# Queueing the joins of the FFN's transposed words behind the weight cast traced last

## The chip, the cores and the metric

The kernel runs on one core of one Trainium2 chip. The metric is the device time of one execution in microseconds (us). An execution starts with the inputs in the chip's memory and ends with the output there. "PE" is TensorE, "DVE" VectorE, "ACT" ScalarE, "POOL" GpSimd and "SP" SyncE, which in this kernel issues the DMAs.

## The reference, cut to what matters

Two layers of an encoder on one sequence of 256 tokens with width 1024 are computed in float32. Each layer has two attention branches, a merge, a gated feed-forward net (FFN) and an embedding per layer. The change touches the FFN alone, whose hidden width is 2816:

```python
u  = rms_norm(h, g_ffn_pre)                 # 256 x 1024
gu = u @ w_ffn_in                           # 256 x 5632: gate | up
h  = h + rms_norm((silu(gate) * up) @ w_ffn_out, g_ffn_post)
```

## The kernel before, in words

**Precision.** A float32 product is made of three products of a reduced type. Each operand is kept as a rounded part ("hi") and the rest ("lo"), and PE adds hi·hi, hi·lo and lo·hi. `split(hi, lo, src)` makes the two parts: ACT casts (L112), DVE subtracts (L108). Each weight of the net passes through it on its way: SP loads a unit of 1 MB into a buffer (raw, two of them; some weights go to "lent" or "big" buffers), ACT casts it to wh, DVE subtracts to wl and thereby frees the raw buffer for the next load, and PE uses both in 12 or 24 matmuls of 128x512. The class `Stream` (`ws`) does this. At most four units are held as wh and wl (`depth`): a cast waits until PE has done with the unit whose buffer it takes, and the casts and subtractions are traced from `done`, that is, right after PE's work on an older unit is traced.

**The FFN.** The hidden width is worked in blocks of 256. The first part makes blocks singly (`block`, a weight for both halves of the tokens). Six blocks are made in three pairs (`pair`, `seven`): the seven products of a fast 2x2 scheme instead of eight. For it DVE makes sums of weights in place in the lent buffers (`add` in `step`, L289). A step n of a pair uses one weight x, y, z, q or a sum of them, so a step needs its load, for some steps one of the sums, a cast and a subtraction. The products themselves are added and subtracted on ACT and DVE (L617, L621, L624, L626). The order of units is the string `FFN = "uu1u2u34u567" "uo12o34o5o67" "poo12o345o67"`: u is a unit of a single block, a digit a step of a pair, o an output unit of w_ffn_out, p the loads for the end of the layer. So the second and the third pair are mixed with output units.

**The transposes.** The hidden values come out as tokens x width, and the output product needs width x tokens. In the FFN this goes by a DMA. `turn_words` copies the 16-bit words of the float32 values apart on ACT (L401), SP issues a transposing DMA (L407), ACT joins the words again in two copies for a block (L413) or in one for half a pair (L419), and `self.put` splits the result (ACT cast, DVE subtraction). It is a generator: a task that runs along. At each `tick()` of the main program the open tasks may go one step on, so the joins are traced some steps after the DMA. There are eleven such transposes in each FFN.

**The order of the work.** The Python program's order isn't the order of the engines' queues. The recorded instructions go through a scheduler of the language, which sets each engine's order by its own estimates of when an operand is ready. Each engine then works through its queue in order and waits at an instruction whose operand isn't there. `tc.issue_after(x)` makes the instructions traced under it stand behind x. On one engine this is a matter of queue order alone, with no semaphore. The kernel uses it in other places already (for instance L442, L469, L526).

In the profile, names like wh_0ffnin stand for all tiles of that kind and part of the program: 0 is the first layer, ffnin the first part of the FFN. Where a text needs one tile, it is told by the number that the program gives it, as in the listings of the change below: wh_0ffnin_2964, or wh_2964 for short.

Of the kernel before, what the change touches and what calls it, by code (L numbers as in the profile page):

```python
# [18 lines left out]
P = 128  # L19
T = 256  # L20
# [30 lines left out]
def trunk_kernel(ctx: ExitStack, tc: tile.TileContext, a: dict, out: bass.AP):  # L51
# [7 lines left out]
    nc = tc.nc  # L59
# [17 lines left out]
    def big(dt=F32):  # L77
        return bigp.tile([P, 2048], dt, tag="big", name=nm("big"))

    def mid(dt=F32):  # L80
        return b4p.tile([P, 1024], dt, tag="mid", name=nm("mid"))
# [7 lines left out]
    def t512():  # L89
        return smp.tile([P, 512], F32, tag="t512", name=nm("t512"), bufs=7)  # L90
# [16 lines left out]
    def vsub(out, in0, in1):  # L107
        nc.vector.tensor_tensor(out=out, in0=in0, in1=in1, op=ALU.subtract)  # L108

    def split(hi, lo, src):  # L110

        nc.scalar.copy(hi, src)  # L112
        vsub(lo, src, hi.bitcast(F32))


    h = cp.tile([P, 2, D], F32, tag="h", name="h")
# [93 lines left out]
    class Stream:  # L210
# [70 lines left out]

        def made(self, x):
            for piece in self.put(x):
                split(*piece)

        def step(self, n, x, y, z, q):
            def add(to, other):
# [18 lines left out]
        def fill(self):  # L306
            while self.open and self.held < self.depth and self.jobs:
                pieces = self.jobs.pop(0)()
                for piece in pieces or ():
                    split(*piece)  # L310
                if pieces:
                    self.load()

# [9 lines left out]
    ws = Stream(4)  # L323
# [36 lines left out]
    class Split:  # L360
# [26 lines left out]
        def put(self, src, k, n, t0, tn):  # L387

            split(*self.at(k, n, t0, tn), src.rearrange("p (k t) -> p k t", t=tn))

        def turn_words(self, src, k, n, hf=None, far=False):

            x = lambda: t512()[:, : n * P * (2 if hf is None else 1)]
            w = x()
            w16 = w.bitcast(U16)  # L400
            nc.scalar.copy(  # L401
                w16.rearrange("p (s c) -> p s c", s=2), src.bitcast(U16).rearrange("p (c s) -> p s c", s=2)
            )
            yield SENT
            r, z = [t[:, : n * P * (2 if hf is None else 1)] for t in halves(mid())] if far else (x(), None)
            r16 = r.bitcast(U16)
            nc.sync.dma_start_transpose(out=r16.rearrange("p (r t) -> p r t", t=P), in_=w16)  # L407
            yield LANDED
            z = x() if z is None else z
            z16 = z.bitcast(U16)  # L410
            if hf is None:
                for i in range(2):
                    nc.scalar.copy(  # L413
                        z16.rearrange("p (k h t s) -> p h s k t", k=2, h=2, s=2)[:, i],
                        r16.rearrange("p (s h k t) -> p h s k t", h=2, k=2, s=2)[:, i],
                    )
                self.put(z, k, n, 0, T)
            else:
                nc.scalar.copy(z16.rearrange("p (c s) -> p s c", s=2), r16.rearrange("p (s c) -> p s c", s=2))  # L419
                self.put(z, k, n, hf * P, P)  # L420

        def tok(self, k, hf):
            return [t[:, 0, :] for t in self.at(k, 1, hf * P, P)]
# [68 lines left out]
    def halves(t):  # L492
        return [t[:, j * 512 : (j + 1) * 512] for j in range(2)]
# [88 lines left out]
    def sums(x):  # L582

        made = []

        def make():  # L590
            yield 1
            (a11, a12), (a21, a22) = x
            s2 = t512()
            vsub(a22, a21, a22)
            vsub(s2, a22, a11)
            nc.vector.tensor_tensor(out=a12, in0=a12, in1=s2, op=ALU.add)
            yield 1
            vsub(a21, a11, a21)
            for s in (a22, s2, a12, a21):
                parts = halves(mid(F32R))  # L600
                split(*parts, s)
                made.append([p.rearrange("p (k t) -> p k t", t=P) for p in parts])
                yield 1

        return made, Task(make(), part[0])

    def seven(sp, forms, gated, last):

        made, task = forms
        quad = lambda hf, j: lambda k: sp.tok(4 * j + k, hf)  # L610
        form = lambda i: lambda k: [p[:, k, :] for p in made[i]]
# [191 lines left out]
    for l in range(DEPTH):  # L803
# [219 lines left out]
        for x in range(2):  # L1023
            o = project_t(uT)
            for i in range(2):
                dst = qk[:, x, 2 * i : 2 * i + 2, :]
                src = o[i].rearrange("p (h t) -> p h t", t=T)
# [165 lines left out]
        for br in range(2):  # L1193
            t = big().rearrange("p (s c) -> p s c", s=2)
# [130 lines left out]
        for x in FFN:  # L1325
# [7 lines left out]
            if x == "o":  # L1333
                n, w = outs.pop(0), ws.take()
# [32 lines left out]
        for hf in range(2):  # L1367
            s = slice(hf * P, (hf + 1) * P)
# [85 lines left out]
```

## Time and profile before

| | us |
|---|---|
| median of three runs | 933.96 |
| the three runs | 930.89, 933.96, 934.84 |
| the profiled execution | 932.07 |
| its span (first to last instruction) | 930.4 |
| PE busy | 911.5 (98%) |
| DVE busy | 721.4 (78%) |
| ACT busy | 622.8 (67%) |

The span is the time from the first to the last instruction that the profiler saw, and the profiled execution took 1.67 us more than that. The FFN of layer 0 lies at about 263 to 440 us, that of layer 1 at 719 to 895 us; the first pair comes at about 300 to 330 us (layer 1: 755 to 785), the second at 330 to 375 and the third at 375 to 415. In rows of a timeline the columns are start, duration, engine, line, operation, out<-in, shape, and in brackets the idle time of the engine before the instruction and what ended it. Rows of waits give the sum, the number of times and the longest. "xN" is a group of N instructions of a kind that follow one another.

### The profile page before, as it was taken

What the parts mean: (1) busy time and instruction counts of PE and PEld (TensorE: products, weight loads), DVE (VectorE), ACT (ScalarE), POOL (GpSimd) and SP (SyncE); (2) the same over time, 40 slices, a digit from 0 to 9 for tenths busy, and PEclk for the clock granted to TensorE, in tenths of its full rate; (3) what the DMA queues carried; (4) which work ended last, traced back from release to release, by engine and by line L of the source; (5) the groups of instructions that cost most, each with busy time, mean ns of one, the idle gap of its engine ahead of it and who ended that gap; (6) DMA issues with size and microseconds to landing.
All of it is one profiled execution on the core that took longest, in us unless ns stands there. A gap on an engine that the chain in (4) does not pass through costs nothing.

```text
span 930.4 us, 12115 instructions
## 1 busy us (share of the span) xinstructions
PE 911.5 (98%) x4577; PEld 770.7 (83%) x4577; DVE 721.4 (78%) x871; ACT 622.8 (67%) x952; POOL 84.6 (9%) x150
## 2 busy tenths in 40 slices
PE   9999999999999989999999999999999998999996
PEld 7998888888878777888899988888888787788786
DVE  5798977656569798898689789665566797989874
ACT  5569678735477776667765686785545876857663
POOL 3500211100000000000123002100001000000000
PEclk9999999999999999999999999999999999999998
DMA  7464456857376665846555525396664856765551
GB/s 250 150 227 135 138 180 179 290 188 211 97 250 212 204 217 185 276 145 239 174 182 181 182 91 161 123 273 214 205 213 143 271 174 203 238 232 174 181 181 46
DMA packets 119896, 177.11 MB, mean 190 GB/s; under 512 B 35159, under 2 KB 58199, under 8 KB 119838
## 3 DMA queue, kind: packets, MB, share of 16 engines
q1 hardware_dynamic: 119838, 176.34, 59.1%
q8 instruction: 36, 0.59, 0.3%
q14 instruction: 22, 0.18, 0.1%
HBM read 167.41 MB, written 1.05 MB: 181 GB/s over the span
## 4 chain that ended last, share of the span: by engine, by line
PE 82%; ACT 5%; DMA 4%; DVE 4%; issue 3%; POOL 2%; SPq 0%; POOLq 0%; DVEq 0%; ACTq 0%
PE acc_1ffnin L96 10%; PE acc_0ffnin L96 9%; PE acc_1ffnin L573 5%; PE acc_1gate L96 5%; PE acc_0gate L96 5%; PE acc_1merge L96 5%; PE acc_0merge L96 5%; PE acc_0ffnin L573 4%; PE acc_1gqk L96 2%; PE acc_0gqk L96 2%; PE acc_0rq L96 2%; PE acc_1ple L96 2%; PE acc_0gg L96 2%; PE acc_1gg L96 2%; PE acc_1v L96 2%
## 5 line engine op out<-in xcount | busy, mean ns | idle before, releaser
L96 PE MATMUL acc_1ffnin<-wh_1ffnin,big_1ffnin 128*128 128x512 f32 x176 | 56.6, 392 | 0.0
L96 PE MATMUL acc_0ffnin<-wh_0ffnin,big_0ffnin 128*128 128x512 f32 x176 | 56.1, 391 | 0.0
L108 DVE TENSOR_TENSOR wl_1ffnin<-raw_1ffnin,wh_1ffnin 128x1024 fp32r<-128x1024 f32 (+1 forms) x26 | 43.9, 1713 | 6.5 <-ACT wh_1ffnin L112 6.4
L108 DVE TENSOR_TENSOR wl_0ffnin<-raw_0ffnin,wh_0ffnin 128x1024 fp32r<-128x1024 f32 (+1 forms) x26 | 43.8, 1713 | 6.0 <-ACT wh_0ffnin L112 5.6
L112 ACT CAST wh_0ffnin<-raw_0ffnin 128x1024 fp32r<-128x1024 f32 (+1 forms) x26 | 36.8, 1450 | 16.7 <-DMA raw_0ffnin<-in_w_ffn_out_dram 14.1
L112 ACT CAST wh_1ffnin<-raw_1ffnin 128x1024 fp32r<-128x1024 f32 (+1 forms) x26 | 37.0, 1447 | 16.1 <-DMA raw_1ffnin<-in_w_ffn_out_dram 6.9
L108 DVE TENSOR_TENSOR wl_0ffnin<-lent_0ffnin,wh_0ffnin 128x2048 fp32r<-128x2048 f32 (+1 forms) x19 | 34.6, 1839 | 7.9 <-ACT wh_0ffnin L112 7.9
L108 DVE TENSOR_TENSOR wl_1ffnin<-lent_1ffnin,wh_1ffnin 128x2048 fp32r<-128x2048 f32 (+1 forms) x19 | 34.6, 1838 | 7.8 <-ACT wh_1ffnin L112 7.8
L96 PEld LDWEIGHTS acc_1ffnin<-wh_1ffnin,big_1ffnin 128*128 128x128 f32 x176 | 33.0, 188 | 7.1 <-ACT big_1ffnin L112 0.2
L96 PEld LDWEIGHTS acc_0ffnin<-wh_0ffnin,big_0ffnin 128*128 128x128 f32 x176 | 33.0, 188 | 7.1 <-ACT big_0ffnin L112 0.3
L112 ACT CAST wh_0ffnin<-lent_0ffnin 128x2048 fp32r<-128x2048 f32 (+1 forms) x19 | 29.2, 1551 | 8.1 <-DVE lent_0ffnin L289 3.3
L96 PE MATMUL acc_1ffnin<-wl_1ffnin,big_1ffnin 128*128 128x512 f32 x88 | 34.3, 390 | 0.0
L96 PE MATMUL acc_0ffnin<-wl_0ffnin,big_0ffnin 128*128 128x512 f32 x88 | 34.2, 390 | 0.0
L112 ACT CAST wh_1ffnin<-lent_1ffnin 128x2048 fp32r<-128x2048 f32 (+1 forms) x19 | 29.1, 1549 | 7.5 <-DVE lent_1ffnin L289 3.1
L573 PE MATMUL acc_0ffnin<-wh_0ffnin,mid_0ffnin 128*128 128x512 f32 x96 | 31.3, 392 | 0.6 <-ACT wh_0ffnin L112 0.6
L573 PE MATMUL acc_1ffnin<-wh_1ffnin,mid_1ffnin 128*128 128x512 f32 x96 | 31.3, 392 | 0.5 <-ACT wh_1ffnin L112 0.5
L96 PE MATMUL acc_0ffnin<-wh_0ffnin,big_0wout 128*128 128x512 f32 x96 | 30.4, 390 | 0.0
L96 PE MATMUL acc_1ffnin<-wh_1ffnin,big_1wout 128*128 128x512 f32 x96 | 30.4, 389 | 0.0
L108 DVE TENSOR_TENSOR wl_1gate<-raw_1gate,wh_1gate 128x1024 fp32r<-128x1024 f32 x14 | 16.5, 1222 | 15.2 <-ACT wh_1gate L112 15.2
L108 DVE TENSOR_TENSOR wl_0gate<-raw_0gate,wh_0gate 128x1024 fp32r<-128x1024 f32 x14 | 17.2, 1273 | 11.8 <-ACT wh_0gate L112 11.7
L573 PE MATMUL acc_1ffnin<-wh_1ffnin,big_1wout 128*128 128x512 f32 x72 | 23.5, 392 | 2.5 <-DVE mid_1ffnin L108 2.5
L573 PE MATMUL acc_0ffnin<-wh_0ffnin,big_0wout 128*128 128x512 f32 x72 | 23.5, 392 | 2.4 <-DVE mid_0ffnin L108 2.3
(659 smaller groups left out, 2970.2 us busy)
## 6 DMA issues: line engine op xcount, KB each, us to landing
raw_0ffnin<-in_w_ffn_out_dram SPq DMA_DIRECT2D x11, 1024.0 KB, 5.6
raw_1ffnin<-in_w_ffn_out_dram SPq DMA_DIRECT2D x11, 1024.0 KB, 4.9
lent_0ffnin<-in_w_ffn_in_dram SPq DMA_DIRECT2D x6, 1024.0 KB, 7.4
lent_1ffnin<-in_w_ffn_in_dram SPq DMA_DIRECT2D x6, 1024.0 KB, 5.8
raw_0rq<-in_w_in_dram SPq DMA_DIRECT2D x4, 1024.0 KB
raw_0v<-in_w_in_dram SPq DMA_DIRECT2D x4, 1024.0 KB
raw_0gg<-in_w_in_dram SPq DMA_DIRECT2D x4, 1024.0 KB, 5.0
raw_0gate<-in_w_o_gla_dram SPq DMA_DIRECT2D x4, 1024.0 KB, 5.3
```

What stands on the lines that cost most here:

```text
L96: return nc.tensor.matmul(o, lhsT, rhs, start=start, stop=stop)
L108: nc.vector.tensor_tensor(out=out, in0=in0, in1=in1, op=ALU.subtract)
L112: nc.scalar.copy(hi, src)
L573: nc.tensor.matmul(o, x, y, start=first and k + n == 0, stop=k == 3 and n == 2, skip_group_check=not first)
```

## The change

`split` returns its ACT cast, and `Stream` keeps the cast of the last weight unit traced (`ws.cast`). In `turn_words` the joins and the split behind them are traced under `tc.issue_after(ws.cast.ins)`, where `far` is set, which is the case for the FFN's transposes. No instruction is added or taken away.

```diff
     def split(hi, lo, src):
-        nc.scalar.copy(hi, src)
+        cast = nc.scalar.copy(hi, src)
         vsub(lo, src, hi.bitcast(F32))
+        return cast
...
         def made(self, x):
             for piece in self.put(x):
-                split(*piece)
+                self.cast = split(*piece)
...
                 for piece in pieces or ():
-                    split(*piece)
+                    self.cast = split(*piece)
...
             z16 = z.bitcast(U16)
-            if hf is None:
-                for i in range(2):
-                    nc.scalar.copy(...)
-                self.put(z, k, n, 0, T)
-            else:
-                nc.scalar.copy(...)
-                self.put(z, k, n, hf * P, P)
+            with tc.issue_after(ws.cast.ins) if far else nullcontext():
+                if hf is None:
+                    for i in range(2):
+                        nc.scalar.copy(...)
+                    self.put(z, k, n, 0, T)
+                else:
+                    nc.scalar.copy(...)
+                    self.put(z, k, n, hf * P, P)
```

The lines of the program move by one or two (L413 is L415 in the changed kernel, L419 is L421, L289 is L290). The scheduler changes the orders of ACT, DVE and PE at several places of both FFNs, in both layers alike. The numbers of the tiles are the same in both programs.

Place A: ACT's queue in layer 0 at the first pair's steps 6 and 7. wh_2931 is the cast of step 6, wh_2964 that of step 7, wh_2968 that of a single block's unit, wh_3011 that of an output unit; mid_2922 holds the words of a single block. Before:

```order
L112 CAST wh_0ffnin_2931<-raw_0ffnin_2796 128x2048
L413 COPY mid_0ffnin_2922<-mid_0ffnin_2922 128x2x2x128 x2
L112 CAST wh_0ffnin_2964<-lent_0ffnin_2589 128x2048
L112 CAST big_0ffnin_2882<-mid_0ffnin_2922 128x2x256
L112 CAST wh_0ffnin_2968<-raw_0ffnin_2889 128x2048
L112 CAST wh_0ffnin_3011<-raw_0ffnin_2962 128x2048
```

And with the change:

```order
L112 CAST wh_0ffnin_2931<-raw_0ffnin_2796 128x2048
L112 CAST wh_0ffnin_2964<-lent_0ffnin_2589 128x2048
L112 CAST wh_0ffnin_2968<-raw_0ffnin_2889 128x2048
L415 COPY mid_0ffnin_2922<-mid_0ffnin_2922 128x2x2x128 x2
L112 CAST wh_0ffnin_3011<-raw_0ffnin_2962 128x2048
L112 CAST big_0ffnin_2882<-mid_0ffnin_2922 128x2x256
```

The two join copies have moved from ahead of two weight casts to behind them, and their own cast to big_2882 behind a third.

Place B: DVE's queue in layer 0 at the second pair's steps 3 to 6. wl_3141 is step 3, wl_3161 step 4, wl_3195 an output unit, wl_3214 step 5, wl_3232 the next output unit, wl_3262 step 6; the line L289 or L290 into lent_2972 with raw_3117 makes the sum for step 7; big_3136 and big_3191 are parts of transposed hidden values. Before:

```order
L108 TENSOR_TENSOR big_0ffnin_3136<-mid_0ffnin_3050,big_0ffnin_3136 128x4x128
L108 TENSOR_TENSOR big_0ffnin_3136<-mid_0ffnin_3064,big_0ffnin_3136 128x4x128
L108 TENSOR_TENSOR wl_0ffnin_3141<-lent_0ffnin_2972,wh_0ffnin_3140 128x2048
L108 TENSOR_TENSOR wl_0ffnin_3161<-big_0ffnin_2974,wh_0ffnin_3160 128x2048
L108 TENSOR_TENSOR big_0ffnin_3191<-mid_0ffnin_3105,big_0ffnin_3191 128x2x256
L108 TENSOR_TENSOR wl_0ffnin_3195<-raw_0ffnin_3015,wh_0ffnin_3194 128x2048
L289 TENSOR_TENSOR lent_0ffnin_2972<-lent_0ffnin_2972,raw_0ffnin_3117 128x2048
L108 TENSOR_TENSOR wl_0ffnin_3214<-lent_0ffnin_2976,wh_0ffnin_3213 128x2048
L108 TENSOR_TENSOR mid_0ffnin_3120<-acc_0ffnin_3122,mid_0ffnin_3120 128x512
L108 TENSOR_TENSOR wl_0ffnin_3232<-raw_0ffnin_3198,wh_0ffnin_3231 128x2048
L108 TENSOR_TENSOR wl_0ffnin_3262<-raw_0ffnin_3117,wh_0ffnin_3261 128x2048
L108 TENSOR_TENSOR mid_0ffnin_3119<-mid_0ffnin_3119,acc_0ffnin_3121 128x512
```

And with the change:

```order
L108 TENSOR_TENSOR big_0ffnin_3136<-mid_0ffnin_3050,big_0ffnin_3136 128x4x128
L108 TENSOR_TENSOR wl_0ffnin_3141<-lent_0ffnin_2972,wh_0ffnin_3140 128x2048
L290 TENSOR_TENSOR lent_0ffnin_2972<-lent_0ffnin_2972,raw_0ffnin_3117 128x2048
L108 TENSOR_TENSOR big_0ffnin_3136<-mid_0ffnin_3064,big_0ffnin_3136 128x4x128
L108 TENSOR_TENSOR wl_0ffnin_3161<-big_0ffnin_2974,wh_0ffnin_3160 128x2048
L108 TENSOR_TENSOR big_0ffnin_3191<-mid_0ffnin_3105,big_0ffnin_3191 128x2x256
L108 TENSOR_TENSOR wl_0ffnin_3195<-raw_0ffnin_3015,wh_0ffnin_3194 128x2048
L108 TENSOR_TENSOR wl_0ffnin_3214<-lent_0ffnin_2976,wh_0ffnin_3213 128x2048
L108 TENSOR_TENSOR mid_0ffnin_3120<-acc_0ffnin_3122,mid_0ffnin_3120 128x512
L108 TENSOR_TENSOR mid_0ffnin_3119<-mid_0ffnin_3119,acc_0ffnin_3121 128x512
L108 TENSOR_TENSOR wl_0ffnin_3232<-raw_0ffnin_3198,wh_0ffnin_3231 128x2048
L108 TENSOR_TENSOR wl_0ffnin_3262<-raw_0ffnin_3117,wh_0ffnin_3261 128x2048
```

The sum with raw_3117 has moved from behind wl_3195 to ahead of big_3136's second half and wl_3161, and the subtraction into mid_3119 from behind wl_3262 to ahead of wl_3232. The third pair has the same exchange between wl_3457 (step 3), the sum of lent_3288 with raw_3338 and wl_3477 (step 4).

On ACT, the stretch beside place B now reads like this, from step 3's cast (wh_3140) to that of the output unit (wh_3194), with step 4's cast (wh_3160) between:

```order
L112 CAST wh_0ffnin_3140<-lent_0ffnin_2972 128x2048
L421 COPY mid_0ffnin_3064<-mid_0ffnin_3064 128x2x512
L112 CAST wh_0ffnin_3160<-big_0ffnin_2974 128x2048
L112 CAST big_0ffnin_3136<-mid_0ffnin_3064 128x4x128
L415 COPY mid_0ffnin_3105<-mid_0ffnin_3105 128x2x2x128 x2
L112 CAST wh_0ffnin_3194<-raw_0ffnin_3015 128x2048
```

Before, the three copies stood ahead of wh_3140, and only one cast of hidden values (big_3191 from mid_3105) stood between wh_3160 and wh_3194. PE's order there changes too: four matmuls of the output unit (wh_3194) stand after step 3 and the first matmul of step 4, ahead of the rest of step 4; before, they stood behind all of step 4.

More of the change, by code (lines that the diff above doesn't have):

```diff
@@ L410, in turn_words @@
             z16 = z.bitcast(U16)
-            if hf is None:
-                for i in range(2):
[L413 to L416, printed above, removed]
-                self.put(z, k, n, 0, T)
-            else:
-                nc.scalar.copy(z16.rearrange("p (c s) -> p s c", s=2), r16.rearrange("p (s c) -> p s c", s=2))
-                self.put(z, k, n, hf * P, P)
+            with tc.issue_after(ws.cast.ins) if far else nullcontext():
+                if hf is None:
+                    for i in range(2):
+                        nc.scalar.copy(
+                            z16.rearrange("p (k h t s) -> p h s k t", k=2, h=2, s=2)[:, i],
+                            r16.rearrange("p (s h k t) -> p h s k t", h=2, k=2, s=2)[:, i],
+                        )
+                    self.put(z, k, n, 0, T)
+                else:
+                    nc.scalar.copy(z16.rearrange("p (c s) -> p s c", s=2), r16.rearrange("p (s c) -> p s c", s=2))
+                    self.put(z, k, n, hf * P, P)
         def tok(self, k, hf):
```

## The prediction

> **What bounds the kernel now.** I read the page's busy table first, then the waits of PE, then the timelines of the places at which PE waited.
>
> ```profile
> span 930.4 us, 12115 instructions
> PE 911.5 (98%) x4577; PEld 770.7 (83%) x4577; DVE 721.4 (78%) x871; ACT 622.8 (67%) x952; POOL 84.6 (9%) x150
> ```
>
> PE is busy for 98% of the span, so no change of order can win more than the time in which PE waits. The waits of PE (line, releaser: us in total, times, longest) say where these are:
>
> ```profile
> PE acc_1ffnin L573 <- DVE mid_1ffnin L108: 2.5, 1, 2.5
> PE acc_0ffnin L573 <- DVE mid_0ffnin L108: 2.3, 1, 2.3
> ...
> PE acc_0ffnin L573 <- ACT wh_0ffnin L112: 0.6, 1, 0.6
> ...
> PE acc_1ffnin L573 <- ACT wh_1ffnin L112: 0.5, 1, 0.5
> ```
>
> All four lie in the two FFNs, where joins, casts and subtractions share ACT and DVE. I call the first kind stall A and the second stall B.
>
> **Stall A.** The timeline at the first pair's steps 6 and 7 in layer 0, rows of all engines:
>
> ```profile
> 315.38 0.50 PE L96 MATMUL acc_0ffnin<-wl_0ffnin,big_0wout 128*128 128x512 f32 x1 [0.17 <-DVE wl_0ffnin L108]
> ...
> 320.49 0.39 PE L96 MATMUL acc_0ffnin<-wh_0ffnin,big_0wout 128*128 128x512 f32 x1
> ...
> 322.43 1.40 ACT L413 COPY mid_0ffnin<-mid_0ffnin 128x512 uint16<-128x512 uint16 x2 [3.87 <-DMA mid_0ffnin<-t_0ffnin]
> 323.70 1.90 ACT L112 CAST wh_0ffnin<-lent_0ffnin 128x2048 fp32r<-128x2048 f32 x1
> ...
> 325.63 2.29 DVE L108 TENSOR_TENSOR wl_0ffnin<-lent_0ffnin,wh_0ffnin 128x2048 fp32r<-128x2048 f32 x1 [4.74 <-ACT wh_0ffnin L112]
> 327.84 0.68 DVE L108 TENSOR_TENSOR mid_0ffnin<-mid_0ffnin,acc_0ffnin 128x512 f32<-128x512 f32 x1
> ...
> 327.95 0.92 SPq L259 DMA_DIRECT2D lent_0ffnin<-in_w_ffn_in_dram  x2
> 328.66 0.47 PE L573 MATMUL acc_0ffnin<-wh_0ffnin,big_0wout 128*128 128x512 f32 x1 [2.34 <-DVE mid_0ffnin L108]
> ```
>
> ACT stood 3.87 us before the join of mid_0ffnin_2922, until the transposing DMA had landed. Queued behind it: step 7's cast wh_2964, DVE's subtraction of it, the small subtraction that frees step 7's accumulator, and SP's loads for the next pair, whose buffer the same subtraction frees.
>
> **Place A after the change.** The casts wh_2964 and wh_2968 stand ahead of this join. wh_2964 can't start at 318.56, when ACT falls idle (322.43 − 3.87), though: it takes a buffer that PE reads until 320.88 (the row at 320.49 and its 0.39). Small waits just before, such as the one at 315.38, go too (a join stood ahead of those casts as well); I put them at 0.45, an estimate, so I start the cast at 320.45, 3.25 earlier than 323.70. Subtraction, accumulator and loads follow by as much: loads at 324.7, and step 7's wait of PE is gone. That is 2.34 of idle and 0.25 of refill, 2.6; with the 0.45, PE is 3.05 ahead. The join now lands in a gap of ACT behind the casts, and its own reader comes over 20 us later: it costs nothing.
>
> **Place B, the second pair's steps 3 and 4 and the out unit behind them:**
>
> ```profile
> 347.49 2.29 DVE L289 TENSOR_TENSOR lent_0ffnin<-lent_0ffnin,big_0ffnin 128x2048 f32<-128x2048 f32 x1
> ...
> 352.46 1.92 ACT L112 CAST wh_0ffnin<-big_0ffnin 128x2048 fp32r<-128x2048 f32 x1
> 352.61 2.29 DVE L108 TENSOR_TENSOR wl_0ffnin<-lent_0ffnin,wh_0ffnin 128x2048 fp32r<-128x2048 f32 x1 [1.64 <-ACT wh_0ffnin L112]
> 353.49 0.39 PE L573 MATMUL acc_0ffnin<-wh_0ffnin,mid_0ffnin 128*128 128x512 f32 x1
> 354.43 0.50 PE L573 MATMUL acc_0ffnin<-wh_0ffnin,mid_0ffnin 128*128 128x512 f32 x1 [0.56 <-ACT wh_0ffnin L112]
> 354.96 0.50 PE L573 MATMUL acc_0ffnin<-wl_0ffnin,mid_0ffnin 128*128 128x512 f32 x1
> 355.30 0.64 PE L573 MATMUL acc_0ffnin<-wh_0ffnin,mid_0ffnin 128*128 128x512 f32 x2
> ```
>
> From 353.49 to 355.30 stand three matmuls that at the usual pitch of 0.227 take 0.68: 1.13 lost. Afterwards, with a DVE that is 3.2 ahead: the sum that step 3 needs ends at 346.5 (it ended at 349.78), wh_3140 is cast until 348.5, wl_3141 is there at 350.85. PE comes at 353.49 − 3.05 = 350.44 and waits 0.3 to 0.4. It then has step 3's matmuls to 353.5 and one of wh_3160, and stands at 353.75 before four of wh_3194. On ACT that cast now comes last of a row: wh_3140 to 348.4, a join of 1.36, wh_3160 to 351.5, a 0.5 cast, the two block joins (1.40 in the row at 322.43), then wh_3194 from 353.25 to 355.17. PE waits 1.5, to 355.25. So B costs 1.85 where it cost 1.13. From there 47 matmuls (12 + 24 + 12 less the one done) lead to wh_3231: 355.25 + 47 × 0.227 = 365.9, against 368.28 before (the four at 368.28 are counted back from the row at 369.41 below). PE is still 2.4 ahead.
>
> **Where this is given back: the out unit wh_3231.**
>
> ```profile
> 357.63 2.28 DVE L108 TENSOR_TENSOR wl_0ffnin<-raw_0ffnin,wh_0ffnin 128x2048 fp32r<-128x2048 f32 x1
> 359.83 2.28 DVE L289 TENSOR_TENSOR lent_0ffnin<-lent_0ffnin,raw_0ffnin 128x2048 f32<-128x2048 f32 x1
> ...
> 359.94 0.37 SPq L259 DMA_DIRECT2D raw_0ffnin<-in_w_ffn_out_dram  x1
> ...
> 365.11 3.72 ACT L112 CAST wh_0ffnin<-raw_0ffnin 128x2048 fp32r<-128x2048 f32 x2 [4.87 <-DMA raw_0ffnin<-in_w_ffn_out_dram]
> 367.05 4.49 DVE L108 TENSOR_TENSOR wl_0ffnin<-raw_0ffnin,wh_0ffnin 128x2048 fp32r<-128x2048 f32 x2 [2.13 <-ACT wh_0ffnin L112]
> ...
> 369.41 0.48 PE L96 MATMUL acc_0ffnin<-wl_0ffnin,big_0ffnin 128*128 128x512 f32 x1
> ```
>
> This is a chain without slack: wl_3195 ends (359.91) and frees a raw buffer, SP issues the load (359.94), 5.17 us later ACT casts, DVE subtracts to 369.34, and PE's first matmul on wl_3232 stands at 369.41. PE's lead is worth what this chain is earlier, and no more. In the new order of DVE the sum lent_2972 += raw_3117 (2.2 by pitch) stands ahead of wl_3195 instead of behind it. So: wl_3141 to 350.85, sum to 353.05, 0.6 for big_3136, wl_3161 to 355.85, 0.6 for big_3191, wl_3195 to 358.7. The load goes out at 358.75, 1.2 earlier and not 3.2. Cast from 363.95 to 365.85; a small subtraction that now stands ahead of wl_3232 waits for PE's accumulator, closed at 365.9 by the 47 matmuls, and takes until 366.75; wl_3232 to 369.05. PE reads it at 369.1: of 2.4 only **0.3** is left. (If the small subtraction did not hold it, 1.2: the other end.)
>
> **The third pair, steps 3 to 5:**
>
> ```profile
> 397.15 1.92 ACT L112 CAST wh_0ffnin<-lent_0ffnin 128x2048 fp32r<-128x2048 f32 x1 [0.20 <-DVE lent_0ffnin L289]
> ...
> 401.30 2.29 DVE L108 TENSOR_TENSOR wl_0ffnin<-big_0ffnin,wh_0ffnin 128x2048 fp32r<-128x2048 f32 x1
> ...
> 404.47 0.39 PE L573 MATMUL acc_0ffnin<-wl_0ffnin,mid_0ffnin 128*128 128x512 f32 x1
> ...
> 418.07 0.62 PE L573 MATMUL acc_0ffnin<-wh_0ffnin,big_0wout 128*128 128x512 f32 x2
> ```
>
> Before, wl_3477 ended at 403.59, 0.88 ahead of PE's use at 404.47. In the new order the sum lent_3288 += raw_3338 and a 0.6 subtraction stand ahead of it (+2.8), while wl_3457 starts some 0.4 to 0.6 earlier (its cast no longer has a join before it, and waits for DVE's sum alone): wl_3477 ends at 405.8 ± 0.15. PE goes on at 405.85 with 58 matmuls to the one that stood at 418.29 (the second of the row at 418.07): 405.85 + 13.17 = 419.0 to 419.1. That is **0.8 later than before** (the lead of 0.3 is in it). Ends: −0.3, if the sum hides after all, and +1.1. The tail of the FFN keeps its chain; I add 0.1.
>
> **Layer 1** has the same orders and the same rows:
>
> ```profile
> 777.67 1.40 ACT L413 COPY mid_1ffnin<-mid_1ffnin 128x512 uint16<-128x512 uint16 x2 [4.17 <-DMA mid_1ffnin<-t_1ffnin]
> ...
> 815.08 0.37 SPq L259 DMA_DIRECT2D raw_1ffnin<-in_w_ffn_out_dram  x1
> ...
> 822.11 4.50 DVE L108 TENSOR_TENSOR wl_1ffnin<-raw_1ffnin,wh_1ffnin 128x2048 fp32r<-128x2048 f32 x2 [2.05 <-ACT wh_1ffnin L112]
> ...
> 856.08 2.28 DVE L108 TENSOR_TENSOR wl_1ffnin<-big_1ffnin,wh_1ffnin 128x2048 fp32r<-128x2048 f32 x1
> ...
> 859.52 0.39 PE L573 MATMUL acc_1ffnin<-wl_1ffnin,mid_1ffnin 128*128 128x512 f32 x1
> ```
>
> The same walk ends at −0.1 to 0 at its out unit, and at +1.0 behind the third pair (wl ends at 860.95 instead of 858.36, PE wanted it at 859.52, and 0.3 to 0.4 of small waits behind it go).
>
> **The sum.** Layer 0: −2.6 − 0.45 (A), +0.7 (B), +2.05 (chain of the out unit), +1.1 (third pair), +0.1 = +0.9. Layer 1: +1.0. Together +1.9 on a span of 930.4. The profiled execution took 932.07 (so 934.0 by this), the median of the runs is 933.96 (935.8). I name **935.0**, between them. No instruction is added or removed, so nothing else is priced.
>
> **Rivals.** (1) *Faster: A and B go and nothing is given back.* For it: both waits are named in the table, and 3.87 and 4.17 us of ACT's waiting go for certain. Against: the out unit's chain, unless its load goes out 3 us earlier. Worth 2 × (2.6 + 1.1) = 7.4: about 926.5 from the median, 924.7 from the profiled execution; half of it, if only one of the two places gives back. The Trainium skill has a rule that speaks for this rival ("DMA: Bandwidth & Descriptors", Rules for kernel authors): issue a DMA early and wait for its semaphore late, with compute between. By that rule the joins were waited for too early, and moving them behind the casts is a pure gain; the row of 3.87 at place A bears it out for that place, and no row says it for what stands behind.
>
> (2) *Slower: a sum that moved ahead on DVE waits for its load.* raw_3117's load is issued when wl_3114 has freed its buffer, about 344.4 in the new run, and the sum would take it at 350.85, 6.4 later.
>
> ```profile
> 345.28 2.28 DVE L108 TENSOR_TENSOR wl_0ffnin<-raw_0ffnin,wh_0ffnin 128x2048 fp32r<-128x2048 f32 x1
> ...
> 347.60 0.37 SPq L259 DMA_DIRECT2D raw_0ffnin<-in_w_ffn_in_dram  x1
> ...
> raw_1ffnin<-in_w_ffn_in_dram SPq DMA_DIRECT2D x1, 1024.0 KB, 5.5
> ...
> lent_0ffnin<-in_w_ffn_in_dram SPq DMA_DIRECT2D x6, 1024.0 KB, 7.4
> ```
>
> The load of this very tile took 5.5 in layer 1, other 1 MB loads with company 7.4 at the median. At 6.4 it decides; at 7.4 to 8 all of DVE behind it, wl_3195 and so the out unit's load slip 1.0 to 1.6. Over two layers and two such sums that is 4 to 6 on top of 935: about 939.5 to 941.
>
> (3) *Nothing to see*: the joins move, but PE's waits are only passed on at once (B grows by what A loses), 934.
>
> **How the numbers follow.** What a measurement of this kernel can tell from no change is about 0.5%, 4.7 us: 929.3 to 938.6. The forecast, gain at A and B spent again at the out unit and the third pair, has 0.65, rival 3 has 0.06, and both are "same": 0.71. Rival 1, whole or large enough to pass the bound, 0.14; rival 2 0.15. The ends of the open terms (out unit −0.9 a layer, third pair −1.1 or +0.3) put the forecast's own range at 930.5 to 937.5. To leave out no more than 2 in 10 it is widened on either side into the rivals: 928 to 939.5.
>
> **What would show it.** Right: ACT's wait before the join of the blocks is gone in both layers, and so is PE's 2.3 and 2.5 at step 7; new waits of PE for wh_3194 (about 1.5) and for wl_3232 (about 1 to 2 in all) and at step 4 of the third pair (about 1.2); the load raw_3198 goes out about 358.7. Wrong towards faster: that load goes out before 357.5, or the sum on DVE is not followed by a wait of PE. Wrong towards slower: DVE waits for a DMA before a sum of L290, which it never does before. If place A keeps its wait of PE, the cause of stall A is read wrongly.

## The result, and the profile after

| | before | changed |
|---|---|---|
| median | 933.31 us (19 runs) | 936.48 us (19 runs) |
| ratio to before, 95% interval | | 1.0034 [1.0023, 1.0046] |
| profiled execution | 932.07 | 937.2 |
| its span | 930.4 | 935.5 |

One of the 19 runs of the changed kernel took 2346.69 us and is left out of the ratio; the median of the other 18 is 936.17. The change costs 3.2 us by the ratio. It lies inside the 0.5% that I called "same", 1.5 us above the forecast of 935.0. The page of the changed kernel answers the busy table like this:

```profile
span 935.5 us, 12107 instructions
PE 913.7 (98%) x4577; PEld 771.1 (82%) x4577; DVE 720.8 (77%) x871; ACT 622.3 (67%) x952; POOL 83.9 (9%) x150
```

The work is the same: only PE is busier, by 2.2. Most of this can be the clock, to which the last section comes; executions without such a fall of the clock show between 908.8 (e4, told below) and 913.3 (e9). The waits of PE in the changed kernel:

```profile
PE acc_1ffnin L96 <- ACT wh_1ffnin L112: 1.3, 1, 1.3
PE acc_0ffnin L96 <- ACT wh_0ffnin L112: 1.2, 1, 1.2
PE acc_0ffnin L575 <- DVE wl_0ffnin L108: 1.0, 3, 0.6
...
PE acc_0ffnin L96 <- DVE wl_0ffnin L108: 0.9, 1, 0.9
...
PE acc_1ffnin L96 <- DVE wl_1ffnin L108: 0.8, 1, 0.8
...
PE acc_0ffnin L575 <- ACT mid_0ffnin L628: 0.5, 1, 0.5
```

The waits of 2.3 and 2.5 for step 7's accumulator are gone from the table. A handful of waits of about 1 us stand in their place. The timeline of the changed kernel shows the places in layer 0, in order of time (columns as before):

```profile
320.73 1.91 ACT L112 CAST wh_0ffnin<-lent_0ffnin 128x2048 fp32r<-128x2048 f32 x1 [2.43 <-PE acc_0ffnin L96]
...
324.99 0.92 SPq L260 DMA_DIRECT2D lent_0ffnin<-in_w_ffn_in_dram  x2
...
325.21 1.41 ACT L415 COPY mid_0ffnin<-mid_0ffnin 128x512 uint16<-128x512 uint16 x2
...
351.45 2.29 DVE L290 TENSOR_TENSOR lent_0ffnin<-lent_0ffnin,raw_0ffnin 128x2048 f32<-128x2048 f32 x1
...
354.26 2.28 DVE L108 TENSOR_TENSOR wl_0ffnin<-big_0ffnin,wh_0ffnin 128x2048 fp32r<-128x2048 f32 x1
...
355.74 1.20 PE L96 MATMUL acc_0ffnin<-wh_0ffnin,big_0ffnin 128*128 128x512 f32 x4 [1.22 <-ACT wh_0ffnin L112]
...
357.06 2.28 DVE L108 TENSOR_TENSOR wl_0ffnin<-raw_0ffnin,wh_0ffnin 128x2048 fp32r<-128x2048 f32 x1
...
359.41 0.37 SPq L260 DMA_DIRECT2D raw_0ffnin<-in_w_ffn_out_dram  x1
...
364.59 3.71 ACT L112 CAST wh_0ffnin<-raw_0ffnin 128x2048 fp32r<-128x2048 f32 x2 [6.08 <-DMA raw_0ffnin<-in_w_ffn_out_dram]
366.78 0.69 DVE L108 TENSOR_TENSOR mid_0ffnin<-mid_0ffnin,acc_0ffnin 128x512 f32<-128x512 f32 x1 [4.63 <-PE acc_0ffnin L575]
367.39 4.49 DVE L108 TENSOR_TENSOR wl_0ffnin<-raw_0ffnin,wh_0ffnin 128x2048 fp32r<-128x2048 f32 x2
...
369.73 0.51 PE L96 MATMUL acc_0ffnin<-wl_0ffnin,big_0ffnin 128*128 128x512 f32 x1 [0.86 <-DVE wl_0ffnin L108]
```

Step 7's cast now starts when PE releases its buffer (320.73), the join copies at 325.21 wait for nothing, and the loads of the lent buffers go out at 324.99 (before 327.95). The FFN of this execution began 0.43 later than that of the one before, so the loads are really 3.4 earlier. But the out unit's load, at 359.41 against 359.94, is only 1.0 earlier with the same correction, and PE reads the out unit's wl at 369.73 (before 369.41): 0.1 earlier. Nearly all of the lead is gone there.

To follow the lead of PE I compare the two traces weight tile by weight tile: the time of the last matmul that uses a tile, in one run minus in the run before. The shift at the first tile of the FFN (wh_2360, 273.3 us) is taken off, since executions start at different times (0.43 in the changed kernel's, 1.11 in e9's, −0.59 in e10's, 0.67 in e5's, −0.50 in e4's, 0.58 in e1's). Negative is earlier than before. The last column is the pair's step 6; its step 7 has the same shifts. Layer 0, in us, for the changed kernel and five of the experiments told below:

| | ahead of step 7 (320.3) | end of step 7 (331.2) | step 3, 2nd pair (357.4) | step 5 (368.1) | out unit (373.6) | step 4, 3rd pair (406.7) | end of 3rd pair (418.1) |
|---|---|---|---|---|---|---|---|
| changed | −0.67 | −3.26 | −3.92 | −2.13 | −0.09 | +1.89 | +1.22 |
| e1_sums | −0.70 | −3.29 | −4.53 | −3.56 | −3.03 | −3.05 | −2.09 |
| e9_sum_second_pair | −0.67 | −3.26 | −4.35 | −3.37 | −2.83 | −0.51 | −1.18 |
| e10_sum_third_pair | −0.05 | −2.64 | −3.62 | −1.81 | +0.22 | +0.49 | +1.48 |
| e5_a_only | −0.71 | −3.29 | −3.54 | −3.32 | −3.56 | −2.90 | −3.31 |
| e4_blocks_sums | −0.66 | −3.25 | −4.32 | −4.10 | −4.21 | −2.77 | −2.66 |

The first row is the whole story of the changed kernel: 3.3 us won by the end of step 7, spent again between step 3 and the out unit, and lost beyond that at the third pair. Layer 1 ends at +3.69. Of this about 1.6 are the clock (at its out unit this execution loses 3.70; e11, the same kernel without a fall of the clock there, loses 2.10). Without it the two FFNs make +1.22 + 2.09 = +3.3, close to the 3.2 of the medians.

### The profile page after: what moved, and what is told of

It reads as the page before. It is cut to its first block, busy times and chain, and to the rows that moved or that the text cites. A ratio compares the mean times of both kernels' runs of the same rounds, so it can differ in the third digit from the quotient of the medians.

```text
span 935.5 us, 12107 instructions
## 1 busy us (share of the span) xinstructions
PE 913.7 (98%) x4577; PEld 771.1 (82%) x4577; DVE 720.8 (77%) x871; ACT 622.3 (67%) x952; POOL 83.9 (9%) x150
## 4 chain that ended last, share of the span: by engine, by line
PE 76%; DVE 9%; ACT 5%; DMA 4%; issue 3%; POOL 2%; SPq 0%; POOLq 0%; DVEq 0%; ACTq 0%
PE acc_1ffnin L96 9%; PE acc_0ffnin L96 8%; PE acc_0gate L96 5%; PE acc_1gate L96 5%; PE acc_1merge L96 5%; PE acc_0merge L96 5%; PE acc_1ffnin L575 3%; PE acc_0ffnin L575 3%; PE acc_1gqk L96 2%; PE acc_0gqk L96 2%; PE acc_0rq L96 2%; PE acc_1ple L96 2%; PE acc_1gg L96 2%; PE acc_0gg L96 2%; PE acc_1v L96 2%
## 5 line engine op out<-in xcount | busy, mean ns | idle before, releaser
L96 PE MATMUL acc_0ffnin<-wh_0ffnin,big_0wout 128*128 128x512 f32 x96 | 30.4, 389 | 0.0
L96 PE MATMUL acc_1ffnin<-wh_1ffnin,big_1wout 128*128 128x512 f32 x96 | 30.4, 389 | 0.0
L96 PE MATMUL acc_0rq<-wh_start,big_start 128*128 128x384 f32 (+1 forms) x96 | 24.9, 344 | 0.8 <-ACT big_start L123 0.8
L96 PE MATMUL acc_1gate<-wh_1gate,big_0ple 128*128 128x512 f32 x80 | 24.8, 389 | 0.0
```

The source lines that it names most:

```text
L96: return nc.tensor.matmul(o, lhsT, rhs, start=start, stop=stop)
```

## The experiments

Each kernel is the changed one with an edit, except where the text says "from the kernel before". Ratios are to the kernel before, measured beside it on the same chip. The medians of the kernel before were 933.08 in the first batch (e1 to e4) and 934.16 in the other two. The theories in the expectations are: *sums*, the forecast's own, by which the loss comes from the sums of L290 that stand further ahead on DVE; *joins*, by which it comes from what the moved joins displace on ACT; and *load*, by which the loads' own timing holds the out unit, whatever DVE's order.

### The sums put back: all, the second pair's, the third pair's

A sum is held behind the last subtraction but one that was traced before it:

```diff
+                with tc.issue_after(self.subs[-2].ins):   # the last weight subtractions
                     add(x, q)
```

For e9 and e10 the hold stands on the second or the third pair's sum alone (`if self.nth % 3 == 2` or `== 0`). In e9 DVE has the sum with raw_3117 behind wl_3195 again, and ACT's queue is the same as in the changed kernel. In e10 the sum with raw_3338 stands behind wl_3513 instead of ahead of wl_3477.

> The changed kernel, with one thing put back: the sum of a pair's step 5 (lent_2972 += raw_3117, lent_3288 += raw_3338) is queued on DVE behind the last subtraction traced before step 5's, as it stood in the kernel before. ACT's order stays that of the changed kernel at places A and B and at the third pair. Theory 'sums' (the gain of place A is real and is spent because the sum stands ahead of subtractions that are wanted sooner): the load raw_3198 goes out at about 358.0 instead of 359.4, wl_3232 ends at about 367.4 instead of 369.7, PE's waits at step 4 of the third pair are gone, and each layer is about 2.2 us shorter than before: 928.8. Rival 'joins' (the gain is spent because joins of the pair now stand between weight casts on ACT): nothing of that changes here, 935.5 to 937. Rival 'load' (whatever the order, the out unit's load ends too late for more): 933 to 935.

Measured: 929.88, ratio 0.9964 [0.9952, 0.9976]. This is near the number of *sums* and far from the other two. The hold stands on the first pair's sum as well, but that is worth nothing here: at the end of step 7 e1 has the lead of the changed kernel (−3.29 and −3.26).

> The changed kernel with the hold on the second pair's sum alone: lent_2972 += raw_3117 stands behind the out unit's subtraction wl_3195, and the small subtraction mid_3119 behind wl_3262, as in the kernel before; every row of ACT is that of the changed kernel, and the first and third pair's sums stand as there. Theory 'sums': from the loads at place A to the load raw_3198 it takes some 2 less than in the changed kernel (32.5 instead of 34.4), PE loses nothing like 2.0 at the out unit, the third pair still costs its 1.3 a layer: about 2 a layer, 932 to 933 on the scale on which the kernel before takes 933.3. If the whole gain of the run with all sums held came from the first pair's sum: no change from the changed kernel, 936.

Measured: 931.47, ratio 0.9972 [0.9962, 0.9982]; the changed kernel beside it had 936.23 (e11 below). Holding the one sum is worth 4.8 us (expected: about 2 a layer). The scheduler moves a few things along with it: the small subtraction into mid_3119 stands behind wl_3262 again, the subtraction into big_3191 behind wl_3195, and PE's four matmuls on wh_3194 behind step 4; their shares are in the 4.8. The timeline of e9 at the second pair:

```profile
352.44 2.29 DVE L108 TENSOR_TENSOR wl_0ffnin<-big_0ffnin,wh_0ffnin 128x2048 fp32r<-128x2048 f32 x1 [0.73 <-ACT wh_0ffnin L112]
...
356.01 2.29 DVE L108 TENSOR_TENSOR wl_0ffnin<-raw_0ffnin,wh_0ffnin 128x2048 fp32r<-128x2048 f32 x1 [0.68 <-ACT wh_0ffnin L112]
...
358.33 0.37 SPq L259 DMA_DIRECT2D raw_0ffnin<-in_w_ffn_out_dram  x1
...
358.82 2.29 DVE L289 TENSOR_TENSOR lent_0ffnin<-lent_0ffnin,raw_0ffnin 128x2048 f32<-128x2048 f32 x1
...
365.33 4.49 DVE L108 TENSOR_TENSOR wl_0ffnin<-raw_0ffnin,wh_0ffnin 128x2048 fp32r<-128x2048 f32 x2 [1.42 <-ACT wh_0ffnin L112]
```

With 0.68 added for e9's later start, wl_3195 starts 1.7 earlier than in the changed kernel (356.01 against 357.06), the load behind it goes out 1.8 earlier (358.33 against 359.41), and wl_3232 starts 2.7 earlier (365.33 against 367.39). The table shows −2.83 instead of −0.09 at the out unit. It also tells what place B waits for. wl_3161, step 4's, starts 2.5 earlier (352.44 against 354.26, with the same correction), and PE takes it without a wait: from step 3 to step 4 e9 loses 0.53, the changed kernel 2.67. The theory *sums* holds for the second pair, for most of the loss.

> The changed kernel with the hold on the third pair's sum alone: lent_3288 += raw_3338 stands behind wl_3513 instead of ahead of wl_3477; places A and B as in the changed kernel. Theory 'sums': PE's waits at step 4 of the third pair go (1.3 a layer), the out unit behind it gives some back: 1 to 1.3 a layer, 934 to 934.5. If the first pair's sum were the whole gain: 936.

Measured: 936.37, ratio 1.0024 [1.0012, 1.0036]. This sum is worth next to nothing, against the expectation: by the traces the third pair costs 1.26 instead of 1.31 in layer 0, and 1.03 instead of 1.72 in layer 1. The table shows how: from the out unit to step 4 the changed kernel loses 1.98, e10 only 0.27, so the wait at step 4 is cured. But 0.99 more is lost from there to the end of the pair, where the changed kernel gains 0.67. DVE in e10, and PE's new wait:

```profile
398.85 2.29 DVE L108 TENSOR_TENSOR wl_0ffnin<-lent_0ffnin,wh_0ffnin 128x2048 fp32r<-128x2048 f32 x1 [1.38 <-ACT wh_0ffnin L112]
...
401.87 2.29 DVE L108 TENSOR_TENSOR wl_0ffnin<-big_0ffnin,wh_0ffnin 128x2048 fp32r<-128x2048 f32 x1 [0.73 <-ACT wh_0ffnin L112]
...
407.48 2.28 DVE L289 TENSOR_TENSOR lent_0ffnin<-lent_0ffnin,raw_0ffnin 128x2048 f32<-128x2048 f32 x1
...
409.69 2.28 DVE L108 TENSOR_TENSOR wl_0ffnin<-raw_0ffnin,wh_0ffnin 128x2048 fp32r<-128x2048 f32 x1
...
412.02 0.50 PE L96 MATMUL acc_0ffnin<-wl_0ffnin,big_0ffnin 128*128 128x512 f32 x1 [0.69 <-DVE wl_0ffnin L108]
```

Up to 412 DVE works almost without a gap but for its two idle times of 1.38 and 0.73, 2.11 in all, so these go straight to the end of the stretch. In the kernel before there was one of 0.78 in the same place:

```profile
399.09 2.29 DVE L108 TENSOR_TENSOR wl_0ffnin<-lent_0ffnin,wh_0ffnin 128x2048 fp32r<-128x2048 f32 x1 [0.78 <-ACT wh_0ffnin L112]
...
408.50 2.29 DVE L108 TENSOR_TENSOR wl_0ffnin<-raw_0ffnin,wh_0ffnin 128x2048 fp32r<-128x2048 f32 x1
```

The stretch from the first of these subtractions to the last takes 10.84 in e10 and 9.41 before: it has the idle 0.73 in it, and the subtraction behind the moved join (0.68), which before was done ahead of the stretch, in the time in which DVE now idles. Wherever the sum stands, something behind it is late. Both idle times end with an ACT cast, so I looked at ACT in the changed kernel:

```profile
397.22 1.91 ACT L112 CAST wh_0ffnin<-lent_0ffnin 128x2048 fp32r<-128x2048 f32 x1 [0.50 <-DVE lent_0ffnin L290]
399.04 1.37 ACT L421 COPY mid_0ffnin<-mid_0ffnin 128x1024 uint16<-128x1024 uint16 x1
400.26 1.90 ACT L112 CAST wh_0ffnin<-big_0ffnin 128x2048 fp32r<-128x2048 f32 x1
```

The moved join of 1.37 stands between the casts wh_3456 and wh_3476, which start 3.04 apart. Before, it stood ahead of both, and they started 1.82 apart (397.15, in the forecast's row, and the next row of ACT):

```profile
398.97 1.90 ACT L112 CAST wh_0ffnin<-big_0ffnin 128x2048 fp32r<-128x2048 f32 x1
```

Here the rows speak for *joins*. In the next group this join comes out of the way, though not alone.

### Parts of the change

The condition `far` decides which joins are held. `hf is None` is a whole block (two join copies), otherwise it is half a pair's words (one copy); k tells which block.

```diff
-            with tc.issue_after(ws.cast.ins) if far else nullcontext():
+            # e2_blocks:     if far and hf is None
+            # e3_pairs:      if far and hf is not None
+            # e5_a_only:     if far and hf is None and k == 10   (mid_2922, place A)
+            # e7_no_block10: if far and (hf is not None or k != 20)
```

e7 leaves out the block's join that ends ahead of wh_3194 at place B.

> The change for the single blocks' joins alone; the joins of the pairs are queued as before. Place A is as in the changed kernel; at place B the pair's joins stand ahead of wh_3140 again. On DVE the sum with raw_3117 stands between wl_3161 and wl_3195, still ahead of the out unit's subtraction, and the small subtraction mid_3119 still ahead of wl_3232; in the third pair the sum stands behind wl_3513. Theory 'sums': A's gain is lost again at the out unit (load at about 358.6, wl_3232 to about 369.3) and nothing is lost at the third pair: 932.5 to 933.5. Rival 'joins': no join among the casts, so the gain of A and B stays: about 927 to 928.5. Rival 'load': 933.

Measured: 930.86, ratio 0.9973 [0.9964, 0.9983]. It lies between the number of *sums* and that of *joins*.

> The change for the pairs' joins alone; the blocks' joins are queued as before, so ACT waits at place A as before. On DVE the sum with raw_3117 stands right behind wl_3141 and the sum with raw_3338 right behind wl_3457, as in the changed kernel. Theory 'sums': no gain at A, wl_3195 and so the load raw_3198 some 1 to 2 later than before, and 1.2 to 1.4 lost at the third pair: 2.5 a layer, 938. Rival 'joins': the same side, but without the blocks' joins between wh_3160 and wh_3194 place B costs about 1 less than in the changed kernel: 937. Rival 'load': 935 (third pair alone).

Measured: 939.71, ratio 1.0065 [1.0053, 1.0077]. The halves of the pairs, moved alone, bring no gain at A and a loss of 6.6 us, more than any of the three numbers expected. The blocks, moved alone, bring a gain.

> The change for one join of each layer alone, that of mid_2922 at place A. ACT's and DVE's orders at place B are those of the kernel before, and the sums stand where they stood; in the third pair the cast wh_3456 stands two places earlier on ACT. Theory 'sums': A's 2.6 stays, since DVE's chain to the out unit's load is ahead by as much and nothing is put into it: load raw_3198 at about 357.2, PE's wait before wl_3232 small, 2.6 to 3 a layer, 927.8. Theory that any gain at A is lost at the out unit because its load can't go out earlier: 932 to 933.

Measured: 926.92, ratio 0.9922 [0.991, 0.9933]. One join out of the eleven in each FFN, moved alone, wins 7.2 us by the medians (5.4 by the shifts at the ends of the two third pairs, −3.31 and −2.11). The timeline of e5 shows the chain of the out unit with the second pair in the order of before:

```profile
325.20 0.92 SPq L260 DMA_DIRECT2D lent_0ffnin<-in_w_ffn_in_dram  x2
...
354.79 2.29 DVE L108 TENSOR_TENSOR wl_0ffnin<-raw_0ffnin,wh_0ffnin 128x2048 fp32r<-128x2048 f32 x1
...
357.11 0.37 SPq L260 DMA_DIRECT2D raw_0ffnin<-in_w_ffn_out_dram  x1
...
364.12 4.49 DVE L108 TENSOR_TENSOR wl_0ffnin<-raw_0ffnin,wh_0ffnin 128x2048 fp32r<-128x2048 f32 x2 [2.04 <-ACT wh_0ffnin L112]
```

From the lent loads to the out unit's load are 31.91 us here (325.20 to 357.11), as in the kernel before (327.95 to 359.94: 31.99). In the changed kernel they are 34.42. So the lead of A is passed on whole from one pair to the next, if nothing in between is reordered. That excludes *load*.

At the third pair of e5, where the joins stand ahead of the casts, there is no join between wh_3456 and wh_3476, and DVE hardly idles:

```profile
392.98 1.91 ACT L112 CAST wh_0ffnin<-lent_0ffnin 128x2048 fp32r<-128x2048 f32 x1
...
395.77 1.94 ACT L112 CAST wh_0ffnin<-big_0ffnin 128x2048 fp32r<-128x2048 f32 x1
...
399.95 2.29 DVE L290 TENSOR_TENSOR lent_0ffnin<-lent_0ffnin,raw_0ffnin 128x2048 f32<-128x2048 f32 x1
```

The lead goes from −3.56 at the out unit to −3.31 at the end of the pair, so the third pair costs 0.25 instead of 1.31. In e4, told below, where the pairs' joins stand ahead as well, it goes from −4.21 to −2.66. But 1.43 of that are lost at the pair's step 2, ahead of this place, where PE waits 1.11 for wl_3401: the lent load at the head of its chain took 8.5 us there (369.56 to 378.04) and 6.8 in the kernel before (374.38 to 381.14). From step 3 to the end e4 loses 0.11.

> The changed kernel without its effect on the block join at place B (mid_3105), which stands ahead of wh_3140 again; the pairs' joins and place A as in the changed kernel, the sums still ahead on DVE, the small subtraction behind wl_3262. The cast wh_3194 comes some 1.3 earlier and PE's wait of 1.6 for it shrinks. Theory 'sums': that is worth nothing, as the load raw_3198 goes out no earlier than 358.8; the small subtraction's 0.9 a layer at most: 934.7 to 936. Rival 'joins' (what stands between the casts on ACT is what costs): 1.3 a layer and more, 932 to 934.

Measured: 932.92, ratio 0.9989 [0.9979, 0.9999]. The forecast put 1.5 us on PE's wait for wh_3194 behind this join. Without the join the wait goes, yet between step 3 and step 5 PE loses +1.91, as much as in the changed kernel (+1.79), at other places: wl_3161, behind the sum, ends at 356.60 there (changed kernel: 356.54). What e7 wins, it wins at the out unit, which costs +0.40 instead of +2.04. The big_3191 subtraction leaves the queue ahead of wl_3195, and the out unit's load goes out 0.9 earlier than in the changed kernel (0.58 by the rows, and e7's FFN began 0.32 later). The small subtraction into mid_3119 also stands behind wl_3262 again, which is worth about as much (0.86 in e6).

```profile
358.83 0.37 SPq L260 DMA_DIRECT2D raw_0ffnin<-in_w_ffn_out_dram  x1
```

This number lies in the range of *joins* (932 to 934) and refutes the *sums* number for e7, though the gain isn't at the wait that *joins* named: what stands on DVE ahead of wl_3195 counts, whether it is a sum or not.

### The best version

e4 moves the blocks' joins only (e2) and holds the sums (e1). e12 moves place A's join only (e5) and holds the sums.

> Both edits of the two runs above: the change for the blocks' joins alone, and the sum of step 5 held behind the out unit's subtraction (second pair) or step 4's or 5's (third pair). Theory 'sums': A's 2.6 and most of B's 1.1 stay, about 3 a layer: 927.3. Rival 'joins': 927 to 928.5, no better than with the blocks' joins alone. Rival 'load': 933.

Measured: 924.70, ratio 0.9909 [0.9896, 0.9922]: faster than both kernels, and 2.6 us better than expected. It is 6.2 us below e2 and 5.2 below e1, so the sums and the joins each cost something, and neither theory holds alone. e1 and e4 have the same sums held and differ in the pairs' joins alone. Between step 3 and step 5 of the second pair e1 loses 0.97 and e4 0.22, at the out unit e1 loses 0.53 and e4 gains 0.11, and from step 3 to the end of the third pair e1 loses 0.94 and e4 0.11 (layer 1: a loss of 1.03 and a gain of 0.20). e4 at the third pair, PE's wait at step 2 first, and then DVE from wl_3457 to the out unit's wl_3531:

```profile
389.66 0.50 PE L575 MATMUL acc_0ffnin<-wl_0ffnin,mid_0ffnin 128*128 128x512 f32 x1 [1.11 <-DVE wl_0ffnin L108]
...
395.99 2.29 DVE L108 TENSOR_TENSOR wl_0ffnin<-lent_0ffnin,wh_0ffnin 128x2048 fp32r<-128x2048 f32 x1 [0.78 <-ACT wh_0ffnin L112]
...
405.41 2.28 DVE L108 TENSOR_TENSOR wl_0ffnin<-raw_0ffnin,wh_0ffnin 128x2048 fp32r<-128x2048 f32 x1
```

And e1, the same two instructions:

```profile
396.40 2.29 DVE L108 TENSOR_TENSOR wl_0ffnin<-lent_0ffnin,wh_0ffnin 128x2048 fp32r<-128x2048 f32 x1 [1.38 <-ACT wh_0ffnin L112]
...
407.24 2.29 DVE L108 TENSOR_TENSOR wl_0ffnin<-raw_0ffnin,wh_0ffnin 128x2048 fp32r<-128x2048 f32 x1
```

The stretch takes 10.84 in e1, as in e10, and 9.42 in e4, as in the kernel before (9.41): the 1.4 go with the pairs' joins.

> The join of place A alone behind the casts, and all three sums held. With place A clear the first pair's hold should be worth nothing more, the second pair's sum stands where it stood anyway, the third pair's goes behind wl_3513: 0 to 1 better than with the join of place A alone, 925.5 to 926.5. If the first pair's hold is worth its 3 to 4 besides: 923.

Measured: 926.46, ratio 0.9924 [0.9909, 0.9938]. Beside e5 (926.92) the hold is worth nothing once the second pair's order is that of before. The intervals of e4, e5 and e12 overlap.

### Controls and single terms

e8 is the hold on the sums alone, from the kernel before.

> The kernel before, with the hold on the sums alone. It moves one sum of each layer, that of the first pair with raw_2796, two places back on DVE, and no other instruction on any engine; the joins stand as before. A control for the runs with that hold: the gain there comes from the joins and the sums together, so 933.1 (within 1). If the hold itself were the gain: below 930.

Measured: 929.62, ratio 0.9958 [0.9944, 0.9972]. As a control it failed: the hold does something by itself. Its order differs from before at the first pair, where the sum lent_2589 += raw_2796 stands two places further back on DVE, behind wl_2886 and the second of the two multiplications of the block's gate. The multiplications give the transpose its data. Its DMA goes out at 313.74, where the kernel before had it at 316.76; 1.69 of that are the executions' different starts, so 1.3 are won. The timeline and the waits of PE of e8:

```profile
313.74 1.84 SPq L408 DMA_TRANSPOSE mid_0ffnin<-t_0ffnin  x1
...
319.26 1.40 ACT L414 COPY mid_0ffnin<-mid_0ffnin 128x512 uint16<-128x512 uint16 x2 [3.73 <-DMA mid_0ffnin<-t_0ffnin]
...
PE acc_1ffnin L574 <- DVE mid_1ffnin L108: 2.1, 1, 2.1
PE acc_0ffnin L574 <- DVE mid_0ffnin L108: 1.5, 1, 1.5
```

So stall A is 0.8 and 0.4 shorter. Over both FFNs the traces show 1.6 of gain (all of it in layer 0), the ratio 3.9; the rest stays open. (A trace is one execution. That of the kernel before took 932.07, 2.1 less than this batch's median of it.) It doesn't touch the reading of e9, whose hold is on the second pair alone.

e6 takes the small subtraction that held wl_3232 in the forecast, and puts it behind the weight subtraction traced last:

```diff
-        times(a, form(3), False, lambda: vsub(p5, p5, a))
+        def fifth():
+            with tc.issue_after(ws.sub.ins):
+                vsub(p5, p5, a)
+        times(a, form(3), False, fifth)
```

> The changed kernel, with the small subtraction mid_3119 of a pair's step 5 queued on DVE behind the last weight subtraction traced before it (behind wl_3262, as in the kernel before). The sums stay ahead as in the changed kernel. The load raw_3198 stays at about 359.4; wl_3232 then ends at about 368.8 instead of 369.7. If this term of the prediction (0.9 a layer) is right and survives the third pair, 934.7; if the third pair's waits take it up, 936 to 936.5. Nothing comes back of the third pair's loss.

Measured: 935.76, ratio 1.0019 [1.0009, 1.0029]. At its place it does what the forecast said: the out unit costs +1.18 instead of +2.04, 0.86 less (the forecast had 0.9). But the same line also holds the first pair's small subtraction, which frees step 7's accumulator: at the end of step 7 the lead is 0.64 instead of 3.26, at step 3 3.11 instead of 3.92. The two cancel, and the out unit ends at −0.15 where the changed kernel has −0.09.

e11 is the changed kernel once more, in the batch of e9 and e10.

> The changed kernel as it is, timed beside the others on one chip: 1.0034 times the kernel before, 936 to 936.5. A control for the two runs above.

Measured: 936.23, ratio 1.0027 [1.0016, 1.0038].

A third raw buffer, which would cut the tie between wl_3195 and the out unit's load, wasn't tried.

## Why the prediction was right, and where it was not

In layer 0 the terms can be set side by side, from the first row of the table of shifts; times of the trace are given with the 0.43 of the later start taken off.

| | forecast | measured |
|---|---|---|
| A and the small waits ahead of it | −2.6 − 0.45 = −3.05 | −3.26 |
| B (end of step 7 to step 5) | +0.7 | +1.13 |
| chain of the out unit | +2.05 | +2.04 |
| third pair and tail | +1.1 + 0.1 | +1.31 |
| sum, layer 0 | +0.9 | +1.22 |

- **Stall A: right.** The lent loads go out at 324.56 (forecast 324.7), and ACT's wait ahead of the blocks' joins is gone in both layers. The 0.45 of small waits, an estimate, was 0.67 in layer 0 and nothing in layer 1. It wasn't the join's doing: e8, which moves no join, shows 0.69 at the same place. So A by itself brought 2.59 (forecast 2.6), and that the whole of the first line comes out close is partly luck.
- **Place B: near in size, and the cause is not the one named.** PE waits for wh_3194 for 1.22 (forecast 1.5). But without that wait e7 loses as much between step 3 and step 5. The wait was only the form that the loss took. In both kernels wl_3161, which step 4 needs next, ends at 356.5 to 356.6, behind the sum; with the sum back (e9) the loss from step 3 to step 5 is 0.98 instead of 1.79, and with the pairs' joins back as well (e4) it is 0.22. So the sum, which the forecast priced only further on, costs here already, and the pairs' joins cost the rest.
- **The out unit: right, and the main term.** Load at 358.98 (forecast 358.75), wl_3232 starts at 366.96 behind the small subtraction, as forecast, and PE takes it at 369.30 (369.1). e9 shows that the sum's place sets it, with the two small subtractions that move along; e6 shows that the one into mid_3119 has 0.86 of it (0.9).
- **The third pair: right in size, wrong in cause.** *This is the step that failed.* It put the price on the sum lent_3288 += raw_3338 ahead of wl_3477. The waits came at step 4 as forecast (0.53 and 0.64, forecast 1.2 in all; the first of them for an ACT copy that stands behind the late casts), but e10 moved that sum back and won nothing. What e10's and e5's rows point to is the idle time of DVE behind the join that moved between wh_3456 and wh_3476. The forecast saw this join leave the place ahead of wh_3456 and counted a gain of 0.4 to 0.6 for it; where it went to was not counted. That the pairs' joins are the cause is shown by e1 and e4, whose edits differ in nothing else: 0.94 against 0.11 from step 3 on, and in layer 1 a loss of 1.03 against a gain of 0.20. That among them it is the join between wh_3456 and wh_3476 is argued from the rows.
  The timeline of PE in the changed kernel at step 4:

```profile
405.51 0.49 PE L575 MATMUL acc_0ffnin<-wh_0ffnin,mid_0ffnin 128*128 128x512 f32 x1 [0.53 <-ACT mid_0ffnin L628]
...
406.64 0.50 PE L575 MATMUL acc_0ffnin<-wl_0ffnin,mid_0ffnin 128*128 128x512 f32 x1 [0.64 <-DVE wl_0ffnin L108]
```

- **Layer 1** was taken as a copy with +1.0, and is +2.09 without the clock's part: its lead at the end of step 7 is 2.67, not 3.05, and its third pair costs 1.72. So the sum is +3.3 where +1.9 was forecast, 0.3 of the difference from layer 0 and 1.1 from layer 1.

**Rival 1** (nothing given back, 7.4) had the right price and the wrong condition. e5, where only place A's join moves, wins 7.2 by the medians. That this is so near is partly luck: rival 1 counted 1.1 a layer for place B, and e5 wins nothing there (−3.29 ahead of it, −3.32 behind). The rule of the Trainium skill that the forecast weighed there ("DMA: Bandwidth & Descriptors", Rules for kernel authors) is to issue a DMA early and to wait for it late. e5 and place A agree with it; the changed kernel as a whole shows what it leaves out, the work that the later wait now stands in front of. **Rival 2** didn't happen: DVE waits for no DMA ahead of a sum of L290 in the changed kernel. **Rival 3**, 934, is excluded by the interval.

## What to carry to other kernels

Moving a wait to a later place in an in-order queue is worth what stood behind it, and costs what it now stands in front of; list both, for each place that it hits, before it is applied to all eleven transposes. Here one place of eleven paid 7 us, and the others took 10 back through chains without slack (a buffer's release, its next load, the cast). Where an engine works almost without a gap, an idle time put into it comes out at its end wherever the work is shuffled, so ask what made it idle, and not which of its instructions is late.

## What the runs showed of the chip that I had not expected

The granted clock falls for some 3.4 us behind two close waits of PE, in some executions. In the changed kernel, at the out unit of layer 1, PE waits for wh and then for wl, and the windows behind it (window, us, busy time and count of PE, PEld, DVE, ACT, POOL, granted clock, DMA share, GB/s) read:

```profile
824.95 0.51 PE L575 MATMUL acc_1ffnin<-wh_1ffnin,big_1wout 128*128 128x512 f32 x1 [0.60 <-ACT wh_1ffnin L112]
...
826.30 0.55 PE L96 MATMUL acc_1ffnin<-wl_1ffnin,big_1ffnin 128*128 128x512 f32 x1 [0.85 <-DVE wl_1ffnin L108]
...
822.00:826.30 4.30, 2.85 (x11) 1.61 (x9) 2.94 (x3) 4.30 (x3) 0.00 (x0) 1.00 0.00 0
826.30:830.20 3.90, 3.90 (x10) 3.10 (x11) 3.90 (x2) 0.40 (x1) 0.00 (x0) 0.56 0.66 223
830.20:834.00 3.80, 3.80 (x19) 3.09 (x18) 1.18 (x2) 1.91 (x1) 0.00 (x0) 1.00 0.89 330
```

A mean of 0.56 over 3.9 us is what 3.4 us at one half would give (3.9 × 0.44 × 2, an estimate). The window at 0.56 counts 10 matmuls, the next one of nearly the same length 19. About 1.6 us are lost in this way, by the comparison with e11 above, and PE counts as busy in them. It came in four of the fourteen profiled executions (this one, e11 and e2 at layer 0's out unit, e3 at layer 0's third pair), never twice at the same place of the same kernel, and not behind the same pair of waits in layer 0 of this execution. Single waits of 2.3 and 2.5 in the kernel before were followed by no fall. Two short waits cost more here than one long one, now and then; why is not settled. The Trainium skill ("TensorE: Matmul & The Clock Gate", Part 1) has the clock halve after a full idle window of about 3.4 us, in windows that run freely. The fall to about half and its length agree with these rows, but no idle time of 3.4 us stands ahead of it: the two waits are 0.60 and 0.85.
